# The high parts of the mixers' weight pieces come by a transfer from HBM that casts, and two loads use another queue

## The chip, the cores and the metric

The kernel runs on one core of one Trainium2 chip. TensorE (PE in the profile) multiplies, VectorE (DVE) and ScalarE (ACT) do elementwise work, GpSimd (POOL) does little here besides starting transfers, and SyncE (SP) starts most transfers. Each of these engines has a queue of its own that it works off in order; semaphores join them. The metric is the device time of one execution in microseconds, as the median of several runs; lower is better.

## What is computed

Two layers of a backbone over 256 latent tokens with 256 context tokens ahead of them, 1024 wide. Each layer applies three mixers to one normalised and modulated input `u`, merges them and adds an MLP. Cut to the frame:

```python
for l in range(DEPTH):                      # 2 layers
    u  = rms_norm(h, norm1_g[l]) * (1.0 + sc1) + sh1          # latent, 256 tokens
    uc = rms_norm(hc, norm1_g[l]) * (1.0 + sc1c) + sh1c       # context, 256 tokens
    a_x, a_g, b_q, b_f, b_i, b_o, c_qkv, m_g = split_projection(u @ w_in[l])
    ya = rglru_branch(a_x, a_g, ...)        # gated linear recurrence
    yb = hgrn2_branch(b_q, b_f, b_i, b_o, ...)
    yc = neighbourhood_attention(axial_rope(q_l), axial_rope(k_l), v_l, ..., na_rpb[l])
    h = h + gt1 * merge_branches(ya, yb, yc, m_g, w_branch[l], w_out[l])
    h = h + gt2 * sq_relu_ffn(rms_norm(h, norm2_g[l]) * (1.0 + sc2) + sh2, ffn_w1[l], ffn_w2[l])
    # the context stream takes the same steps in all layers but the last
return h
```

All inputs are float32, and the products are wanted in close to float32 accuracy.

## The kernel before

**Weights.** All weights of the matrix products are packed in HBM as 296 pieces of 128 x 1024 float32 (512 KB), 148 for each layer. A piece passes through three buffers on the chip. `arriving` starts its transfer into `raw` on SyncE's queue (line 211, three buffers). `weights` takes a buffer for the high part `whi` and one for the low part `wlo` (four each), and `split` fills them: ScalarE rounds `raw` to the format that TensorE reads in one pass, `whi` (line 226), and VectorE subtracts, `wlo = raw - whi` (line 227). Each product is then three matmuls with the split input, whi x xhi, whi x xlo and wlo x xhi (`mm3`, lines 240 to 242; in the `tok` pieces lines 1036 to 1038). So the third matmul of a piece is the first that needs `wlo`.

**Pieces and heads.** A layer's mixers are worked off in four heads j = 0 to 3. A head uses ten pieces: `ff` and `fb` (forget gates of hgrn), `hq` (its query), `ax` and `ag` (the linear recurrence's input and gate), `og` (output gate), and `tok` in four parts, tok0 to tok3 (values, and attention's q, k, v). Token tiles and parts of `tok` are worked off in the order of `TOK_UNITS`. The chains that follow the projections (`hgrn`, `attention`, `lru`) are generators in three lanes whose steps are laid between the matmuls of the next head's pieces. Pieces are fetched up to four ahead of the one in use, since there are four `whi` and `wlo` buffers: a new high part can be written as soon as the piece four ahead of it has been used for the last time.

**Order.** The program text gives each piece's steps and a scheduler puts the instructions of each engine in their final order; the queues keep that order. The tables and costs of the planner aren't touched.

**Two other loads.** `opened` in `mixer_pieces` starts, for each head, the load of attention's position bias (`bias`, 512 KB, line 969, on GpSimd's queue but for the very first, on SyncE's) and of the recurrence's gate weights (`gw`, 256 KB, line 977, on GpSimd's queue). `sc` (line 754) first reads the bias.

Of the kernel before, what the change touches and what calls it, by code (L numbers as in the profile page):

```python
# [10 lines left out]
F32 = mybir.dt.float32  # L11
# [5 lines left out]
ALU = mybir.AluOpType  # L17
# [9 lines left out]
NPIECE = 148  # L27
# [9 lines left out]
MIX_ORDER = ("tok", "ff", "fb", "hq", "ax", "ag", "og")  # L37
# [34 lines left out]
def piece_index():  # L72
    idx, n = {}, 0

    def add(key):
        nonlocal n
        idx[key] = n
        n += 1

    for j in range(4):  # L80
        for nm in MIX_ORDER:
            for key in mix_keys(nm, j):
                add(key)
    for _, br, what, i in merge_order(0):
        add((what, br, i))
    for d in range(8):
        add(("out", d))
    for q in range(4):
        for i in range(8):
            add(("f1", q, i))  # L90
    for q in range(4):
        for d in range(8):
            add(("f2", q, d))
    assert n == NPIECE
    return idx


PIECE = piece_index()
# [56 lines left out]
def hybrid_kernel(  # L155
    ctx: ExitStack, tc: tile.TileContext, xT, cT, wpack, ada0w, adaw, lastw, prm, lruw, biasd, consts, cs, gfr, masks, out
):
    nc = tc.nc
# [13 lines left out]
    def two_k(name, dt=F32):  # L172
        return wk.tile([P, T2], dt, tag="t2", name=name, bufs=N2)

    def four_k(name, shape=(2, T2), dt=F32):
        return wk.tile([P] + list(shape), dt, tag="t4", name=name, bufs=N4)
# [32 lines left out]
    def arriving(l, key):  # L209
        raw = wpool.tile([P, 1024], F32, tag="raw", name="raw", bufs=3)  # L210
        nc.sync.dma_start(out=raw, in_=wpack[l * NPIECE + PIECE[key]])
        return raw

    def weights(l, key, raw=None, eng=nc.vector):
        cols = {"tok": 4 * P, "proj": 2 * P}.get(key[0], P)
        raw = arriving(l, key) if raw is None else raw
        lo = wpool.tile([P, 1024], F32R, tag="wlo", name="wlo", bufs=4)
        hi = wpool.tile([P, 1024], F32R, tag="whi", name="whi", bufs=4)
        split(hi, lo, raw, eng=eng)
        v = lambda t: t.rearrange("p (k c) -> p k c", c=cols)  # L220
        return v(hi), v(lo)

    def split(hi, lo, src, scale=None, eng=nc.vector):

        if scale is None:
            nc.scalar.copy(hi, src)  # L226
            eng.tensor_tensor(out=lo, in0=src, in1=hi.bitcast(F32), op=ALU.subtract)  # L227
        else:
            nc.scalar.mul(hi, src, scale)
            nc.vector.scalar_tensor_tensor(  # L230
                out=lo, in0=src, scalar=scale, in1=hi.bitcast(F32), op0=ALU.mult, op1=ALU.subtract
            )
# [86 lines left out]
    def rope_tables(l):  # L319

        for sc in range(2):
            for i, qk in enumerate((1, 0)):
                g = gf[l][:, 2 * sc + qk, :]
                for hd in range(2):
                    for tt in range(2):
                        nc.gpsimd.tensor_tensor(out=ctab[:, sc, tt, i, hd, :], in0=cst[:, sc, tt, :], in1=g, op=ALU.mult)
# [616 lines left out]
    def mixer_pieces(l):  # L943
        T = T2 if l == 0 else TL
        heads = []
        for j in range(4):
            out_pieces = []
            heads.append(out_pieces)
            m = State()
# [6 lines left out]
            def opened(nm, m=m, j=j):  # L956

                if j == 0 and not hasattr(st, "layer" + str(l)):
                    setattr(st, "layer" + str(l), True)
                    st.ys = {}  # L960
                if nm in ("ff", "fb") and not hasattr(m, "TF"):
                    m.TF = four_k("TF")
                if nm == "hq":
                    m.Q = two_k("Q")
                if nm == "tok" and j == 0 and l > 0:
                    rope_tables(l)
                if nm == "tok":
                    m.bias = four_k("bias", (4, TL))
                    (nc.gpsimd if l or j else nc.sync).dma_start(out=m.bias, in_=biasd[l, j])

                    m.tok = [four_k("tok", (2, 2, TL)) for _ in range(2)]
                    m.vtok = lambda c: m.tok[c // 2][:, 0, c % 2]
                if nm == "og" and not hasattr(m, "sog"):
                    m.sog = two_k("sog")
                if nm in ("ax", "ag") and not hasattr(m, "gw"):
                    m.gw = two_k("gw").rearrange("p (a b) -> p a b", b=P)
                    nc.gpsimd.dma_start(out=m.gw, in_=lruw[l, j])
                    m.xc, m.ge = two_k("xc"), two_k("ge")

            def closed(nm, m=m, j=j, lane=lane, chain=chain):  # L980
# [299 lines left out]
    def start():  # L1280
# [23 lines left out]
        def split_part(i, eng=nc.vector):  # L1304
            if i not in st.first and i < 4:
                st.first[i] = weights(0, ("tok", 0, i), first[i], eng)
# [114 lines left out]
    def fetch(n):  # L1421
        while len(ready) < n and pos[0] < len(todo):
            l, key = todo[pos[0]]
            ready.append(weights(l, key))
            pos[0] += 1
# [146 lines left out]
```

## Time and profile before

| what | value |
|---|---|
| time, median of three runs | 1531.65 us (1529.93 to 1533.64) |
| the profiled execution's own time | 1531.65 us |
| its span in the profile | 1529.9 us |
| TensorE busy | 1513.1 us, 99% |
| VectorE busy | 1120.1 us, 73% |
| ScalarE busy | 762.0 us, 50% |
| GpSimd busy | 27.7 us, 2% |
| mean granted TensorE clock | 0.998 |
| read from HBM | 214.74 MB |

The span runs from the first to the last instruction; 1.75 us of the execution's time lie outside it. A busy share is an average over all stages. TensorE is hardly ever idle, so the end of the program is its queue plus what it waits for; the waits and the timeline tell where it does. The mixers of layer 0 lie at about 62 to 400 us, those of layer 1 at about 950 to 1250; merge, output projection and MLP fill the rest.

### The profile page before, as it was taken

The numbers are of one execution on the slowest core, as the hardware profiler recorded it, in microseconds if no ns is written. First come the engines' busy times: TensorE is split into PE (matmuls) and PEld (weight loads), VectorE is DVE, ScalarE is ACT, GpSimd is POOL, SyncE is SP. The second block draws the span as 40 slices with busy tenths as digits, with TensorE's granted clock in tenths as the row PEclk, the third lists the DMA queues.
The fourth block names the chain that finished last, engine by engine and source line by source line (L and its number), as shares of the span: only waits on it lengthen the run. The fifth ranks groups of instructions, "written<-read, shape, count | busy, mean of one in ns | idle before, by whom it ended". The sixth has DMA issues, their size and how long they took to land.

```text
span 1529.9 us, 24126 instructions
## 1 busy us (share of the span) xinstructions
PE 1513.1 (99%) x9521; PEld 1295.8 (85%) x9522; DVE 1120.1 (73%) x2126; ACT 762.0 (50%) x1269; POOL 27.7 (2%) x57
## 2 busy tenths in 40 slices
PE   9999999999999999999999999999999999999999
PEld 5778787777888889888888888878888899999999
DVE  6777768685478898988695856779687766776664
ACT  3467676757333333532322323576777854454442
POOL 1200000020000000000000000000000000000000
PEclk9999999999999999999999999999999999999999
DMA  9412131221273562555464532313323355755553
GB/s 368 156 42 104 56 104 56 69 76 70 83 260 126 205 222 69 179 187 185 162 210 137 193 110 90 124 63 124 103 71 106 109 166 191 266 164 182 186 183 125
DMA packets 61793, 217.36 MB, mean 142 GB/s; under 512 B 7792, under 2 KB 9456, under 8 KB 61680
## 3 DMA queue, kind: packets, MB, share of 16 engines
q1 hardware_dynamic: 59328, 209.88, 40.2%
q0 software_dynamic: 1648, 5.77, 1.2%
q8 instruction: 75, 1.23, 0.3%
q14 instruction: 38, 0.31, 0.1%
q10 hardware_dynamic: 704, 0.17, 0.1%
HBM read 214.74 MB, written 1.05 MB: 141 GB/s over the span
## 4 chain that ended last, share of the span: by engine, by line
PE 90%; DVE 5%; ACT 4%; issue 1%; DMA 1%; SPq 0%; ACTq 0%
PE pd L240 7%; PE pd L242 7%; PE pd L241 7%; PE pf L240 5%; PE pf L242 5%; PE pf L241 5%; PE pg L240 4%; PE pg L241 4%; PE pg L242 4%; PE ptok L1036 3%; PE ptok L1038 2%; PE ptok L1037 2%; PE pp L240 2%; PE pp L241 2%; PE pp L242 2%; PE lv L547 2%
## 5 line engine op out<-in xcount | busy, mean ns | idle before, releaser
L226 ACT CAST whi<-raw 128x1024 fp32r<-128x1024 f32 x296 | 309.6, 1049 | 464.1 <-PE pd L241 155.7
L227 DVE TENSOR_TENSOR wlo<-raw,whi 128x1024 fp32r<-128x1024 f32 x295 | 360.3, 1223 | 151.7 <-ACT whi L226 149.2
L242 PE MATMUL pd<-hhi,wlo 128*128 128x256 f32 (+1 forms) x544 | 177.8, 327 | 0.0
L240 PE MATMUL pd<-hhi,whi 128*128 128x256 f32 (+1 forms) x544 | 177.8, 327 | 0.0
L241 PE MATMUL pd<-hlo,whi 128*128 128x256 f32 (+1 forms) x544 | 177.7, 327 | 0.0
L354 DVE CUSTOM_DVE_ANT_0 junk<-arow,crow 128x1024 bf16<-128x1024 f32 x144 | 173.4, 1221 | 3.4 <-DMA arow<-in_adaw 3.2
L241 PE MATMUL pf<-xlo,whi 128*128 128x256 f32 (+1 forms) x464 | 155.1, 334 | 0.0
L242 PE MATMUL pf<-xhi,wlo 128*128 128x256 f32 (+1 forms) x464 | 155.0, 334 | 0.0
L240 PE MATMUL pf<-xhi,whi 128*128 128x256 f32 (+1 forms) x464 | 155.0, 334 | 0.0
L240 PE MATMUL pg<-xhi,whi 128*128 128x512 f32 (+1 forms) x384 | 131.5, 342 | 0.0
L241 PE MATMUL pg<-xlo,whi 128*128 128x512 f32 (+1 forms) x384 | 129.6, 337 | 0.0
L242 PE MATMUL pg<-xhi,wlo 128*128 128x512 f32 (+1 forms) x384 | 129.2, 337 | 0.0
L1154 DVE SCALAR_TENSOR_TENSOR h<-pd,mod,h 128x256 f32<-128x256 f32 x120 | 55.0, 481 | 80.7 <-PE pd L242 78.7
L241 PEld LDWEIGHTS pd<-hlo,whi 128*128 128x128 f32 x544 | 103.5, 190 | 8.8
L240 PEld LDWEIGHTS pd<-hhi,whi 128*128 128x128 f32 x544 | 103.5, 190 | 8.7
L242 PEld LDWEIGHTS pd<-hhi,wlo 128*128 128x128 f32 x544 | 103.5, 190 | 8.7
L241 PEld LDWEIGHTS pf<-xlo,whi 128*128 128x128 f32 x464 | 88.3, 190 | 8.7
L242 PEld LDWEIGHTS pf<-xhi,wlo 128*128 128x128 f32 x464 | 88.2, 190 | 8.8
L240 PEld LDWEIGHTS pf<-xhi,whi 128*128 128x128 f32 x464 | 88.1, 190 | 8.6
L1036 PE MATMUL ptok<-whi,xhi 128*128 128x512 f32 (+1 forms) x224 | 87.6, 395 | 1.1 <-DVE h L1154 1.1
L1038 PE MATMUL ptok<-wlo,xhi 128*128 128x512 f32 (+1 forms) x224 | 85.0, 379 | 1.6 <-DVE wlo L227 1.6
L1037 PE MATMUL ptok<-whi,xlo 128*128 128x512 f32 (+1 forms) x224 | 84.6, 378 | 0.2 <-DVE xlo L463 0.2
(329 smaller groups left out, 3271.7 us busy)
## 6 DMA issues: line engine op xcount, KB each, us to landing
raw<-in_wpack SPq DMA_DIRECT2D x296, 512.0 KB, 3.5
arow<-in_adaw SPq DMA_DIRECT2D x72, 512.0 KB, 4.7
a<-in_ada0w SPq DMA_DIRECT2D x16, 512.0 KB, 10.4
araw<-in_lastw SPq DMA_DIRECT2D x8, 512.0 KB, 6.4
bias<-in_biasd POOLq DMA_DIRECT2D x7, 512.0 KB, 6.6
h<-in_xT SPq DMA_DIRECT2D x4, 512.0 KB, 5.5
gw<-in_lruw POOLq DMA_DIRECT2D x8, 256.0 KB, 2.9
out<-h SPq DMA_DIRECT2D x8, 128.0 KB, 1.9
```

The source lines that it names most:

```text
L226: nc.scalar.copy(hi, src)
L227: eng.tensor_tensor(out=lo, in0=src, in1=hi.bitcast(F32), op=ALU.subtract)
L240: nc.tensor.matmul(d, lhsT=whi[:, k, :], rhs=xhi, start=(k == 0), stop=False)
L241: nc.tensor.matmul(d, lhsT=whi[:, k, :], rhs=xlo, start=False, stop=False)
L242: nc.tensor.matmul(d, lhsT=wlo[:, k, :], rhs=xhi, start=False, stop=(k == nk - 1))
L354: nc.vector.tensor_tensor_reduce(out=junk, in0=raw, in1=crow[s], scale=1.0, scalar=0.0, op0=ALU.mult, op1=ALU.add, accum_out=section_of(l, ...
L547: nc.tensor.matmul(dst, lhsT=lhs(b), rhs=rhs(b), start=True, stop=True)
L1036: nc.tensor.matmul(dst, lhsT=xhi[:, k, tsl], rhs=whi[:, kk, :], start=(k == 0), stop=False)
L1037: nc.tensor.matmul(dst, lhsT=xlo[:, k, tsl], rhs=whi[:, kk, :], start=False, stop=False)
L1038: nc.tensor.matmul(dst, lhsT=xhi[:, k, tsl], rhs=wlo[:, kk, :], start=False, stop=(k == KD - 1))
L1154: nc.vector.scalar_tensor_tensor(out=h[:, d, sl], in0=p_[:, sl], scalar=mods(l, section, s)[:, d:d + 1], in1=h[:, d, sl], op0=ALU.mult, op ...
```

## The change

For the mixers' pieces of all heads but the first of layer 0, `weights` no longer calls `split`. GpSimd's queue starts a transfer that reads the same 512 KB from HBM once more and writes `whi`, of the other type, so that the transfer casts. VectorE's subtraction stays; it now waits for two transfers instead of one transfer and ScalarE. These are 30 pieces in layer 0 and 40 in layer 1, 70 of 296. Besides, all loads of `bias` and `gw` are started on SyncE's queue. The new lines shift the line numbers behind them by 5: the subtraction in the mixers is L222, the one in `split` L232, the third matmul in `tok` L1043.

```diff
--- before.py
+++ after.py
@@ -216,7 +216,12 @@
         raw = arriving(l, key) if raw is None else raw
         lo = wpool.tile([P, 1024], F32R, tag="wlo", name="wlo", bufs=4)
         hi = wpool.tile([P, 1024], F32R, tag="whi", name="whi", bufs=4)
-        split(hi, lo, raw, eng=eng)
+        if key[0] in MIX_ORDER and (l, key[1]) > (0, 0):
+
+            nc.gpsimd.dma_start(out=hi, in_=wpack[l * NPIECE + PIECE[key]])
+            eng.tensor_tensor(out=lo, in0=raw, in1=hi.bitcast(F32), op=ALU.subtract)
+        else:
+            split(hi, lo, raw, eng=eng)
         v = lambda t: t.rearrange("p (k c) -> p k c", c=cols)
         return v(hi), v(lo)
 
@@ -966,7 +971,7 @@
                     rope_tables(l)
                 if nm == "tok":
                     m.bias = four_k("bias", (4, TL))
-                    (nc.gpsimd if l or j else nc.sync).dma_start(out=m.bias, in_=biasd[l, j])
+                    nc.sync.dma_start(out=m.bias, in_=biasd[l, j])
 
                     m.tok = [four_k("tok", (2, 2, TL)) for _ in range(2)]
                     m.vtok = lambda c: m.tok[c // 2][:, 0, c % 2]
@@ -974,7 +979,7 @@
                     m.sog = two_k("sog")
                 if nm in ("ax", "ag") and not hasattr(m, "gw"):
                     m.gw = two_k("gw").rearrange("p (a b) -> p a b", b=P)
-                    nc.gpsimd.dma_start(out=m.gw, in_=lruw[l, j])
+                    nc.sync.dma_start(out=m.gw, in_=lruw[l, j])
                     m.xc, m.ge = two_k("xc"), two_k("ge")
 
             def closed(nm, m=m, j=j, lane=lane, chain=chain):
```

The change moves instructions, since the scheduler orders the engines anew. Two places on VectorE follow; a name's ending number is the program's own and the same on both sides.

The first is VectorE's queue in layer 1 between heads 0 and 1, where the lows of tok1 (`wlo_9410`) and tok2 (`wlo_9471`) of head 1 are subtracted; `xc` is the recurrence's convolution, `kcT` and `qT` attention's keys and queries, `QQ`, `blk`, `km` and `Tn` belong to hgrn, `ge` is the gate's GELU. Before:

```order
L227 TENSOR_TENSOR wlo_9410<-raw_9408,whi_9411 128x1024 [waits DMAHW1_49,Activation_49]
L924 SCALAR_TENSOR_TENSOR xc_9343<-xpre_9403,prb_83,xc_9343 128x2x254 [waits Activation_49]
L230 SCALAR_TENSOR_TENSOR kcT_9427<-kqT_9430,prb_83,kcT_9427 128x256 [waits Activation_49]
L924 SCALAR_TENSOR_TENSOR xc_9343<-xpre_9403,prb_83,xc_9343 128x2x255 [waits DVE_49]
L230 SCALAR_TENSOR_TENSOR qT_9429<-kqT_9430,qg8_654,qT_9428 128x256 [waits Activation_49]
L924 SCALAR_TENSOR_TENSOR xc_9343<-xpre_9403,prb_83,xc_9343 128x2x255 [waits DVE_49]
L560 COPY km_9457<-KK_9363 128x256
L598 TENSOR_TENSOR QQ_9364<-QQ_9364,TF_9171 128x128x2 [waits PE_49]
L601 COPY_PREDICATED blk_9370<-msk_76,lv_9451 128x128
L611 TENSOR_TENSOR Tn_9461<-TF_9171 128x512
L227 TENSOR_TENSOR wlo_9471<-raw_9469,whi_9472 128x1024 [waits DMAHW2_49,Activation_49]
L934 SCALAR_TENSOR_TENSOR ge_9344<-ge_9344,gpre_9463 128x256 [waits Activation_49]
```

Now:

```order
L929 SCALAR_TENSOR_TENSOR xc_9343<-xpre_9403,prb_83,xc_9343 128x2x254 [waits Activation_49]
L929 SCALAR_TENSOR_TENSOR xc_9343<-xpre_9403,prb_83,xc_9343 128x2x255 [waits DVE_49]
L235 SCALAR_TENSOR_TENSOR kcT_9427<-kqT_9430,prb_83,kcT_9427 128x256 [waits Activation_49]
L929 SCALAR_TENSOR_TENSOR xc_9343<-xpre_9403,prb_83,xc_9343 128x2x255 [waits DVE_49]
L222 TENSOR_TENSOR wlo_9410<-raw_9408,whi_9411 128x1024 [waits DMAHW3_49,DMASW3_49]
L235 SCALAR_TENSOR_TENSOR qT_9429<-kqT_9430,qg8_654,qT_9428 128x256 [waits Activation_49]
L565 COPY km_9457<-KK_9363 128x256
L603 TENSOR_TENSOR QQ_9364<-QQ_9364,TF_9171 128x128x2 [waits PE_49]
L606 COPY_PREDICATED blk_9370<-msk_76,lv_9451 128x128
L616 TENSOR_TENSOR Tn_9461<-TF_9171 128x512
L222 TENSOR_TENSOR wlo_9471<-raw_9469,whi_9472 128x1024 [waits DMAHW6_49,DMASW4_49]
L939 SCALAR_TENSOR_TENSOR ge_9344<-ge_9344,gpre_9463 128x256 [waits Activation_49]
```

The low of tok1 moved behind three steps of the convolution and `kcT`, and its wait is for two transfers; the low of tok2 stays between `Tn` and `ge`, with a wait for two transfers instead of one and ScalarE.

The second is VectorE's queue on the way into layer 1, where the lows of tok1 to tok3 of head 0 are `wlo_8328`, `wlo_8334` and `wlo_8340`; `ut` and `xlo` are the modulated input and its low part, `r_g110` and `r_g111` the two token groups' norm scales, `sums` the sum of squares, line 1154 the addition to the residual `h` (now 1159). Before:

```order
L227 TENSOR_TENSOR wlo_8328<-raw_8326,whi_8329 128x1024 [waits DMAHW5_49,Activation_49]
...
L459 SCALAR_TENSOR_TENSOR ut_8290<-h_84,A_g110_8217,rst_8259 128x256
L420 TENSOR_TENSOR sums_7882<-sums_7882,sqt_8295 128x256 [waits Activation_49]
L1154 SCALAR_TENSOR_TENSOR h_84<-pd_8050,mod0_85,h_84 128x256 [waits PE_49]
L463 SCALAR_TENSOR_TENSOR xlo_7881<-ut_8290,mod1_86,xhi_7880 128x256 [waits Activation_49]
L227 TENSOR_TENSOR wlo_8334<-raw_8332,whi_8335 128x1024 [waits DMAHW6_49]
L420 TENSOR_TENSOR sums_7882<-sums_7882,sqt_8323 128x256 [waits Activation_49]
L227 TENSOR_TENSOR wlo_8340<-raw_8338,whi_8341 128x1024 [waits DMAHW7_49]
L488 TENSOR_SCALAR r_g111_8399<-nss_8396 128x2 [waits PE_49]
```

Now:

```order
L1159 SCALAR_TENSOR_TENSOR h_84<-pd_8050,mod0_85,h_84 128x256 [waits PE_49]
L468 SCALAR_TENSOR_TENSOR xlo_7881<-ut_8286,mod1_86,xhi_7880 128x256 [waits Activation_49]
L468 SCALAR_TENSOR_TENSOR xlo_7881<-ut_8290,mod1_86,xhi_7880 128x256 [waits Activation_49]
L425 TENSOR_TENSOR sums_7882<-sums_7882,sqt_8323 128x256 [waits Activation_49]
L222 TENSOR_TENSOR wlo_8328<-raw_8326,whi_8329 128x1024 [waits DMAHW5_49,DMASW7_49]
L222 TENSOR_TENSOR wlo_8334<-raw_8332,whi_8335 128x1024 [waits DMAHW6_49,DMASW0_49]
L222 TENSOR_TENSOR wlo_8340<-raw_8338,whi_8341 128x1024 [waits DMAHW7_49,DMASW1_49]
L493 TENSOR_SCALAR r_g111_8399<-nss_8396 128x2 [waits PE_49]
```

The low of tok1 moved from the first norm scale, ahead of all `ut` and `xlo` of the first group, to the place directly behind the last `sums`, where the other two follow it without anything between.

## Rows read from the trace of the kernel before

L12 is line 12 of the kernel before. A group of instructions on the page reads: line, engine, operation, out<-in with partitions x elements and type, xcount | busy us, mean ns of one | idle us of the engine just ahead of them, and what ended most of it. In the timeline a bracket gives the idle time ahead of an instruction and what ended it.

**Rows 1.** The page: span; engines' busy time; the cast and the subtraction (columns below).

```profile
span 1529.9 us, 24126 instructions
...
PE 1513.1 (99%) x9521; PEld 1295.8 (85%) x9522; DVE 1120.1 (73%) x2126; ACT 762.0 (50%) x1269; POOL 27.7 (2%) x57
...
L226 ACT CAST whi<-raw 128x1024 fp32r<-128x1024 f32 x296 | 309.6, 1049 | 464.1 <-PE pd L241 155.7
L227 DVE TENSOR_TENSOR wlo<-raw,whi 128x1024 fp32r<-128x1024 f32 x295 | 360.3, 1223 | 151.7 <-ACT whi L226 149.2
```

**Rows 2.** Busy time by stretch: one layer 1 head; the sum over nine mixer stretches.

```profile
core 0: us, PE busy (x) PEld busy (x) DVE busy (x) ACT busy (x) POOL busy (x), PEclk, DMA share, GB/s
...
1060.00:1123.00 63.00, 62.11 (x409) 51.68 (x407) 49.61 (x116) 44.88 (x82) 1.07 (x2) 1.00 0.29 94
...
sum 638.00, PE 631.88 PEld 520.96 DVE 472.73 ACT 429.73 POOL 14.33; mean PE 70.21 PEld 57.88 DVE 52.52 ACT 47.75 POOL 1.59
```

**Rows 3.** TensorE's waits, 965 to 1250: us in total, times, longest.

```profile
PE ptok L1038 <- DVE wlo L227: 1.6, 3, 0.5
PE tp L793 <- ACT s L769: 1.0, 3, 0.3
```

**Rows 4.** Timeline, layer 0: ScalarE's cast, TensorE's wait (start, us, engine, line, operation).

```profile
276.70 1.05 ACT L226 CAST whi<-raw 128x1024 fp32r<-128x1024 f32 x1 [0.93 <-PE ptok L1037]
...
283.61 0.44 PE L793 MATMUL tp<-con,s 128*128 128x128 f32 x2 [1.34 <-ACT s L785]
```

**Rows 5.** Timeline of VectorE: lows of tok2 and tok3 in layer 1.

```profile
1061.86 1.22 DVE L227 TENSOR_TENSOR wlo<-raw,whi 128x1024 fp32r<-128x1024 f32 x1
...
1068.72 1.22 DVE L227 TENSOR_TENSOR wlo<-raw,whi 128x1024 fp32r<-128x1024 f32 x1
```

**Rows 6.** Timeline of ScalarE and TensorE in the same passage.

```profile
1059.17 1.04 ACT L226 CAST whi<-raw 128x1024 fp32r<-128x1024 f32 x1
...
1069.99 0.50 PE L1038 MATMUL ptok<-wlo,xhi 128*128 128x512 f32 x1 [0.55 <-DVE wlo L227]
```

**Rows 7.** DMA issues to landing: windows 881:883, 951:952 and 215:216; then whole span.

```profile
bias<-in_biasd POOLq DMA_DIRECT2D x1, 512.0 KB, 4.3
...
bias<-in_biasd POOLq DMA_DIRECT2D x1, 512.0 KB, 3.8
...
bias<-in_biasd POOLq DMA_DIRECT2D x1, 512.0 KB, 7.9
...
raw<-in_wpack SPq DMA_DIRECT2D x296, 512.0 KB, 3.5
...
bias<-in_biasd POOLq DMA_DIRECT2D x7, 512.0 KB, 6.6
```

**Rows 8.** Timeline on the way into layer 1: VectorE, ScalarE, TensorE.

```profile
954.72 1.22 DVE L227 TENSOR_TENSOR wlo<-raw,whi 128x1024 fp32r<-128x1024 f32 x1
955.85 0.42 DVE L420 TENSOR_TENSOR sums<-sums,sqt 128x256 f32<-128x256 f32 x1
...
954.50 0.42 ACT L418 ACTIVATE sqt<-h 128x256 f32<-128x256 f32 x1 [0.28 <-DVE h L1154]
...
955.03 0.40 PE L1038 MATMUL ptok<-wlo,xhi 128*128 128x512 f32 x1
```

**Rows 9.** Timeline around ff: heads 0 and 1 of layer 1.

```profile
966.76 1.05 ACT L226 CAST whi<-raw 128x1024 fp32r<-128x1024 f32 x1 [0.26 <-PE ptok L1037]
...
972.38 0.40 PE L242 MATMUL pff<-xhi,wlo 128*128 128x512 f32 x1
...
1025.46 1.06 ACT L226 CAST whi<-raw 128x1024 fp32r<-128x1024 f32 x1
...
1032.40 0.40 PE L242 MATMUL pff<-xhi,wlo 128*128 128x512 f32 x1
```

**Rows 10.** Timeline: a bias is issued and first used.

```profile
1099.10 0.53 POOL L969 DMA_DIRECT2D bias<-in_biasd  x1 [11.01 <-DVE ltau L882]
...
1127.42 0.42 DVE L754 CUSTOM_DVE_ANT_0 sc<-sc,bias 128x256 f32<-128x256 f32 x1
```

## The prediction

> **What bounds the kernel now.** I read the page first. TensorE is busy 1513.1 of the 1529.9 us span, so nothing but work on its own queue or an idle stretch ahead of a matmul can move the time [rows 1]. The two operations that the change touches are off that queue: ScalarE's rounding of a piece takes 1049 ns and VectorE's subtraction 1223 ns [rows 1]. Both numbers are large in sum, 70 x 1.049 = 73.4 us of ScalarE's time in the 70 pieces concerned, and neither says anything about the end of the program, since ScalarE is busy half of the span.
>
> So the second view is the busy time by stretch, over the stretches in which the mixers run. The reader is to see how little there is to win: TensorE's busy time is 631.88 of 638.00 us, hence 6.1 us idle in all eight heads and the way into layer 1, at full granted clock (1.00) in each row [rows 2]. VectorE in one layer 1 head is busy 49.61 of 63 us, ScalarE 44.88, so on average both have room [rows 2]. The average hides the place that matters, and the third view, TensorE's waits, names it: in layer 1 there are three waits of 0.5 us for a low part (matmul line L1038 waits for wlo), and three short ones for the softmax activation on ScalarE, 1.0 us together [rows 3]. In layer 0 the one wait of size is for ScalarE, 1.34 us ahead of 283.61 [rows 4]. A low part is late in layer 1, then, once in each of three passages from a head to the next.
>
> The fourth view is the timeline of VectorE in such a passage, 1055 to 1070. From tok2's low to tok3's its operations stand back to back. The low of piece tok2 starts at 1061.86, that of tok3 at 1068.72, and TensorE starts its matmul on the latter at 1069.99 after an idle 0.55 us [rows 5, 6]. Everything that pushes VectorE back between these points pushes TensorE back by the same amount.
>
> **The change part by part.** *Removed:* 70 casts on ScalarE. Where ScalarE ends a wait, this gives time back. In layer 0 the cast at 276.70 takes 1.05 us ahead of the activations that TensorE then waits for [rows 4]. At most that 1.3 us comes back, at least nothing, because VectorE's own results feed the same activations; I take 1.0, the length of the cast. In layer 1 the three waits on ScalarE sum to 1.0 us, and I count none of it, since they come behind the low of tok3 and move with it.
>
> *Added:* 70 transfers of 512 KB on GpSimd's queue, each started when the slot of the high part is free, and a wait for it in front of VectorE's subtraction. Today the high part is there 1.05 us after its slot is free; from now on it is there after D, the time from issue to landing. Behind the waiting subtraction, VectorE's whole queue stands. No row of before shows a casting transfer. The nearest rows are the position-bias loads, the same 512 KB, the same queue, without a cast: 3.8 and 4.3 us for the two that ran alone, 6.6 as the median of seven, the other five of which were issued beside weight pieces, and 7.9 at worst; weight pieces of the same size on SyncE's queue have a median of 3.5 [rows 7]. I take D = 4.3, the longer of the two that ran alone: in the passages the raw piece has landed well ahead of the slot, so that few other bytes move, but a cast is not likely to make it shorter. The ends 3.5 and 6.6 are kept, and 7.9 as the tail.
>
> Where does D cost? For each of the 70 pieces I compared the moment when the slot comes free with the moment when TensorE needs the low part. What hides D and the subtraction (4.3 + 1.2 = 5.5 us) is the work on the pieces fetched before, and nearly everywhere it is longer. Three places are tight.
>
> (a) Piece tok2 in layer 1. ScalarE starts its cast at 1059.17, right when the slot is free (the last matmul of the ag piece on it has just gone), and VectorE starts the low at 1061.86 [rows 5, 6]. The order of VectorE in the changed kernel keeps this low in its place, directly behind Tn and ahead of ge. So with D the subtraction starts at 1059.17 + D, later than now by D - 2.69. At 4.3 that is 1.6 us, at 3.5 it is 0.8, at 6.6 it is 3.9. VectorE is not idle from there to the low of tok3, so TensorE's wait at 1069.99 grows by that. Three passages have this form (heads 0 to 1, 1 to 2, 2 to 3): 3 x 1.6 = +4.8 us.
>
> (b) The way into layer 1. The low of tok1 was done early, between two parts of the scale for the norm. In the new order it stands behind all of them, together with the lows of tok2 and tok3, next to the second scale. TensorE uses it at 955.03 [rows 8]. VectorE reaches the place where it now stands at 954.72 at the latest; without the 1.22 us of the moved subtraction that is 953.5, plus the sum of 0.42 us that now precedes it, so it ends at about 953.5 + 0.4 + 1.2 = 955.1, 0.1 us late. If that sum has to wait for ScalarE's square, which starts at 954.50 and ends at 954.9 in this trace, it ends at about 954.9 + 0.4 + 1.2 = 956.5, late by 1.4. I take +0.7, the middle.
>
> (c) The first piece of the hgrn projections (ff). In head 0 of layer 1 the cast starts at 966.76 and TensorE needs the low at 972.38; the path with D is 966.76 + 4.3 + 1.2 = 972.3, hidden with nothing to spare. In heads 1 to 3 it is 1025.46 + 5.5 = 1031.0 against 1032.40, hidden by 1.4 us [rows 9]. At D = 6.6 this cover is gone: 2.2 us in head 0 and 0.9 in each of the other three, 4.9 in all.
>
> *Moved:* the bias and gate-weight loads go from GpSimd's queue to SyncE's. A bias is issued at 1099.10 and first used at 1127.42, and the gate weights have as much ahead of them [rows 10]; on SyncE's queue they stand among the raw pieces of the same head, each of 3.5 us, so they cost nothing. The cover is the rest of the head's projections on TensorE; without it the price is one load, 6.6 us [rows 7]. *Traffic:* 70 x 0.524 = 36.7 MB more from HBM. In a layer 1 head 10 x 0.524 MB in 63 us is 83 GB/s beside today's 94, and the DMA engines are busy 0.29 of that stretch [rows 2]; doubled, it stays under 0.6. Zero, but it lengthens D when a raw piece is in flight.
>
> The sum: -1.0 + 4.8 + 0.7 + 0 = +4.5 us on the profiled execution. That one took 1531.65 us, 1.75 more than its span, and is also the median of the three runs (1529.93 to 1533.64), so it needs no correction: 1536.1 us.
>
> One rule of the Trainium skill speaks against a D of 4.3. "DMA: Bandwidth & Descriptors", section "Anatomy of one DMA — SWDGE (gpsimd) path", gives a transfer on this path a fixed 2.0 us and bytes over 436 GB/s; for 512 KB this is an estimate of 3.2 us, and the sum by it would be -1.0 + 3 x 0.5 + 0.7 = +1.2 us. No load of this size on that queue is that short here (3.8 and 4.3 alone) [rows 7], so the rows decide; 1532.9 us, which the rule gives, lies in the no-change case below.
>
> **The rivals.** *No change.* If a casting transfer lands like a raw piece does, 3.5 us, place (a) costs 3 x 0.8 = 2.4 and the sum is -1.0 + 2.4 + 0.7 = +2.1: 1533.8 us, within what a measurement of this kernel can't tell from no change (0.2%, 3.1 us). For it speaks that the raw pieces are the same bytes; against it, every bias row [rows 7].
>
> *Faster.* The mechanism: the high part is there before VectorE comes to the low of tok2, so VectorE no longer waits anywhere for ScalarE, and ScalarE, freed of 10 casts in each 63 us, ends its softmax activations earlier. It decides at D = 2.7 us in place (a), or later if VectorE itself arrives later than now. Then the three waits for the lows (1.6 us) and those for ScalarE (1.0 and 1.3) go: -3.9 us, 1527.7 us; no more than the 6.1 us of idle time can come back. Against it: no 512 KB row lands within 2.7 us. For it: ScalarE's freed time reaches further than I can follow by hand.
>
> *Slow transfer.* If casting, or the raw pieces beside it, makes D the 6.6 us of the bias median, (a) costs 3 x 3.9 = 11.7, (c) 4.9, (b) 0.7, less 1.0: +16.3, 1548 us. At 7.9 the same terms are 15.6, 3.5 + 3 x 2.2 = 10.1, 0.7 and -1.0: +25.4, 1557 us. For it speaks that a cast touches every element; against it, that the passages are quiet.
>
> That the change doesn't do what it says can be left out: the new order has 70 transfers into whi on GpSimd's queue and 70 casts fewer on ScalarE.
>
> **How the numbers follow.** Forecast (D from 3.8 to 5.5) 0.35, no change 0.32, faster 0.15, slow transfer 0.18. The forecast's case lies almost wholly beyond 0.2%; a little of it falls within and a little of the no-change case beyond, which cancel. So faster 0.15, same 0.34, slower 0.51. For the range: down to 1527, which takes in most of the faster case and leaves out the one in which more than these waits go; up to 1552, D of about 7.2, which leaves the tail of the slow case out. Its own range for the likeliest case, D from 3.8 to 5.5: (a) 3.3 to 8.4, (b) 0.7, (c) 0 to 1.1, less 1.0, is +3.0 to +9.2 us, 1534.7 to 1540.9.
>
> **What would show it.** Right: in the waits of the changed kernel TensorE's L1038 (now L1043) waits some 2 us for wlo three times in layer 1; VectorE's low of tok2 waits for a transfer there; the transfers into whi take about 4.3 us; the 1.3 us wait at 283.61 is gone. Wrong: VectorE never waits for a transfer in layer 1 (then the no-change or faster case), or waits for it in layer 0 or at pieces ff as well (then the slow one), or TensorE's matmuls themselves get longer, which no term here has.

## The result, and the profile after

| | before | after |
|---|---|---|
| median | 1531.14 us (1529.93 to 1533.64) | 1548.14 us (1543.38 to 1548.55) |
| ratio, 95% interval | | 1.0102 (1.0078 to 1.0125) |
| span of the profiled execution | 1529.9 us | 1541.6 us |
| ScalarE busy | 762.0 us | 698.0 us |
| idle time of TensorE in the nine mixer stretches | 6.1 us | 14.6 us |

The change makes the kernel slower by about 1%. The profiled execution is the quickest of the four after (1543.38 us), so the trace explains 11.7 us of a loss of 12 to 19.

The page of the changed kernel, to be read beside [rows 1]: ScalarE's casts are 226 instead of 296, the 70 lows of the changed pieces stand on a line of their own (L222), and their line names the transfer as what ended the idle time ahead of them. TensorE's busy time has hardly moved (1513.1 before); the span has.

```profile
span 1541.6 us, 24163 instructions
...
PE 1514.8 (98%) x9521; PEld 1296.0 (84%) x9522; DVE 1120.4 (73%) x2126; ACT 698.0 (45%) x1199; POOL 56.5 (4%) x112
...
L231 ACT CAST whi<-raw 128x1024 fp32r<-128x1024 f32 x226 | 236.8, 1049 | 420.3 <-PE pd L246 152.1
...
L222 DVE TENSOR_TENSOR wlo<-raw,whi 128x1024 fp32r<-128x1024 f32 x70 | 85.0, 1220 | 37.4 <-DMA whi<-in_wpack 22.5
...
whi<-in_wpack POOLq DMA_DIRECT2D x70, 512.0 KB, 4.4
```

The same two stretch lines as in [rows 2]. The kernel is later by now, so the first stretch doesn't hold quite the same work, but the sum over the same 638 us does nearly: TensorE's busy time falls from 631.88 to 623.40 us, ScalarE's by 66 us, and the DMA engines' share in a head's stretch rises from 0.29 to 0.48.

```profile
1060.00:1123.00 63.00, 60.05 (x397) 50.20 (x396) 49.58 (x116) 36.29 (x71) 5.26 (x10) 1.00 0.48 161
...
sum 638.00, PE 623.40 PEld 511.22 DVE 468.69 ACT 363.83 POOL 45.09; mean PE 69.27 PEld 56.80 DVE 52.08 ACT 40.43 POOL 5.01
```

TensorE's waits in layer 1, to be read beside [rows 3]. A line gives the sum in microseconds, the number of waits and the longest. The waits for the low of a `tok` piece have grown from 1.6 to 3.6 us in sum, and there are new waits, 1.2 us in sum each, for results of VectorE that have nothing to do with a weight piece: `ks` of hgrn, `qT` of attention.

```profile
PE ptok L1043 <- DVE wlo L222: 3.6, 3, 1.2
PE lv L552 <- DVE ks L534: 1.2, 2, 0.9
PE sc L751 <- DVE qT L235: 1.2, 3, 0.5
PE tp L798 <- ACT s L774: 1.0, 3, 0.3
```

VectorE's waits over the whole span name the source: 21 waits for a casting transfer, up to 3.3 us long, and 7 for which the profile shows no releaser.

```profile
DVE wlo L222 <- DMA whi<-in_wpack: 22.5, 21, 3.3
...
DVE wlo L222 <- issue: 5.2, 7, 1.7
```

These two lines don't hold all of it. Of the 37.4 us of idle time that the page gives ahead of these 70 lows, 36.5 us, in 32 waits, end within 0.1 us behind the landing of the low's own transfer; the 7 without a releaser are among them, and so are four that the view puts down to TensorE, which ended something at the same moment. Ahead of the same 70 lows VectorE had stood idle for 16.9 us in the kernel before.

To see where the time went, the start of each of TensorE's matmuls in the trace of after was set against the same matmul of before. The lag grows as follows (us; the place is the time in the trace of before):

| up to | after | queues only | layer 0 only | layer 1 only | layer 1 without tok2 | five buffers |
|---|---|---|---|---|---|---|
| 60, start-up | 0.5 | 0.1 | 0.2 | 1.0 | 2.7 | 0.1 |
| 320, layer 0's mixers | 4.5 | 0.1 | 2.1 | 1.0 | 2.7 | -0.8 |
| 985, way into layer 1 | 5.4 | 0.1 | 2.4 | 3.9 | 5.8 | -1.4 |
| 1255, layer 1's mixers | 12.7 | 0.0 | 2.3 | 10.1 | 12.8 | -1.0 |
| 1525, end | 11.2 | 0.0 | 0.8 | 8.6 | 11.3 | -2.0 |

The columns behind the first belong to experiments below. Two amounts in it aren't the change: what stands in the first row (loading at the start, which no edit here touches, differs from execution to execution), and what all but one of the columns get back at 1340 to 1360, where the execution of before, and not they, lost some clock (1.0 to 1.5 us, below). For after there remain 4.0 us in layer 0, about 1 on the way into layer 1 and 7.3 in layer 1.

### The profile page after: what moved, and what is told of

Read it like the earlier page. It is cut to its first block, busy times and chain, and to the rows that moved or that the text cites. A ratio compares the mean times of both kernels' runs of the same rounds, so it can differ in the third digit from the quotient of the medians.

```text
span 1541.6 us, 24163 instructions
## 1 busy us (share of the span) xinstructions
PE 1514.8 (98%) x9521; PEld 1296.0 (84%) x9522; DVE 1120.4 (73%) x2126; ACT 698.0 (45%) x1199; POOL 56.5 (4%) x112
## 4 chain that ended last, share of the span: by engine, by line
PE 69%; issue 16%; DVE 7%; DMA 4%; ACT 2%; POOL 1%; POOLq 0%; SPq 0%; DVEq 0%; ACTq 0%
PE pd L245 7%; PE pd L247 7%; PE pd L246 7%; PE pf L245 5%; PE pf L247 5%; PE pf L246 5%; PE pg L245 4%; PE pg L247 4%; PE pg L246 4%; DMA whi<-in_wpack 4%; PE pp L246 2%; PE pp L247 2%; PE pp L245 2%; DVE wlo L222 1%; PE ptok L1012 1%
## 5 line engine op out<-in xcount | busy, mean ns | idle before, releaser
L231 ACT CAST whi<-raw 128x1024 fp32r<-128x1024 f32 x226 | 236.8, 1049 | 420.3 <-PE pd L246 152.1
L232 DVE TENSOR_TENSOR wlo<-raw,whi 128x1024 fp32r<-128x1024 f32 x225 | 275.2, 1224 | 133.9 <-ACT whi L231 132.4
L222 DVE TENSOR_TENSOR wlo<-raw,whi 128x1024 fp32r<-128x1024 f32 x70 | 85.0, 1220 | 37.4 <-DMA whi<-in_wpack 22.5
L1043 PE MATMUL ptok<-wlo,xhi 128*128 128x512 f32 (+1 forms) x224 | 84.5, 378 | 3.6 <-DVE wlo L222 3.6
```

The source lines that it names most:

```text
L222: eng.tensor_tensor(out=lo, in0=raw, in1=hi.bitcast(F32), op=ALU.subtract)
L1043: nc.tensor.matmul(dst, lhsT=xhi[:, k, tsl], rhs=wlo[:, kk, :], start=False, stop=(k == KD - 1))
```

## The experiments

Theory A: the casting transfer comes too late. It can't start before a slot of the high part is free, and it takes some 4 us where ScalarE took 1; VectorE's subtraction waits for it at the head of an in-order queue, and all that stands behind it comes late. Theory B: the moved loads. Theory C: the second reading of the weights. Theory D: the new order of VectorE's queue by itself.

**The queue change alone.**

```diff
-                    (nc.gpsimd if l or j else nc.sync).dma_start(out=m.bias, in_=biasd[l, j])
+                    nc.sync.dma_start(out=m.bias, in_=biasd[l, j])
-                    nc.gpsimd.dma_start(out=m.gw, in_=lruw[l, j])
+                    nc.sync.dma_start(out=m.gw, in_=lruw[l, j])
```

> Only the two loads (bias, gw) move to SyncE's queue; ScalarE casts all pieces as before. Theory A (VectorE's queue stands still until casting transfers land): nothing to wait for here, so 1531 us, within 1.5 us of the kernel before. Theory B (the moved loads, 768 KB per head on the raw pieces' queue, are what delays things): raw pieces and high parts late, 4 us or more slower, 1535 or above.

Measured: 1531.67 us, ratio 0.9996 (0.9986 to 1.0006), and a lag within 0.2 us all the way. The two loads cost nothing on the other queue. Theory B falls as a cause by itself.

**The casting transfers alone.** The change without the lines above, so that `bias` and `gw` stay on GpSimd's queue.

> The 70 casting transfers alone; bias and gw stay on GpSimd's queue, where the casting transfers now stand too. Theory A: as slow as the full change, 11 to 17 us over the kernel before (1542 to 1548); the transfers beside bias and gw take as long as there (6 to 7 us for the og pieces), since the bytes move at the same time from either queue. Theory B: 5 us over at most (1536). A third way: bias and gw wait for buffers in the middle of GpSimd's queue and hold the casting transfers behind them, then it is slower than the full change, above 1550.

Measured: 1542.48 us, ratio 1.0071 (1.0053 to 1.0089): slower by 8 to 14 us. So the casting transfers make the loss, together with the order that the scheduler made for them (VectorE's is that of the full change but for a few instructions), and the loads don't hold them up on GpSimd's queue. One part was missed: the transfers of the og pieces, for which 6 to 7 us were expected, take 3.7 to 5.4 us in layer 1 here. Whether the full change (1.0078 to 1.0125) is really some microseconds worse than this one can't be said: the intervals overlap.

**Layer 0 only, layer 1 only.**

```diff
-        if key[0] in MIX_ORDER and (l, key[1]) > (0, 0):
+        if key[0] in MIX_ORDER and l == 0 and key[1] > 0:
```

> Casting transfers for the 30 pieces of layer 0 only; the loads moved as in the change. Theory A, from the lag of TensorE's matmuls against the kernel before at the end of layer 0's mixers in the trace of the changed kernel (4.6 us): 1535 to 1537. The prediction's own term for layer 0 was -1.0: 1530.

Measured: 1535.84 us, ratio 1.0025 (1.0012 to 1.0039).

```diff
-        if key[0] in MIX_ORDER and (l, key[1]) > (0, 0):
+        if key[0] in MIX_ORDER and l == 1:
```

> Casting transfers for the 40 pieces of layer 1 only; the loads moved as in the change. Theory A, from the growth of the lag from the start of layer 1's mixers to their end (4.6 to 12.7 us): 8 us over, 1538 to 1541. The prediction's own terms for layer 1 (4.8 and 0.7): 1536.6. If the lags of the two layers only add in part, this and the layer 0 kernel together give less or more than the full change.

Measured: 1542.66 us, ratio 1.0071 (1.0052 to 1.0090). Layer 0 costs 2 to 6 us where the prediction had a gain of 1; layer 1 costs 8 to 14 where it had 5.5. Their sum, 0.96%, is about the full change's 1.02%.

**Layer 1 without the tok2 pieces.** The prediction put 4.8 of its 5.5 us on three pieces. Here they alone go back to ScalarE.

```diff
-        if key[0] in MIX_ORDER and (l, key[1]) > (0, 0):
+        if key[0] in MIX_ORDER and l == 1 and (key[1] == 0 or key[0] != "tok" or key[2] != 2):
```

> As the layer 1 kernel, but the tok2 pieces of heads 1 to 3, on which the prediction put 4.8 of its 5.5 us for layer 1, are cast by ScalarE again: 37 casting transfers; VectorE's order is the same in both kernels. By the prediction's term the loss of layer 1 all but goes: 1532 to 1533. If the loss is made at the lows ahead of tok2 (ag, og, tok0, tok1), where VectorE's queue stands up to 3 us for a transfer, it stays: 1539 to 1543, as the layer 1 kernel (1542.7).

Measured: 1543.05 us, ratio 1.0063 (1.0041 to 1.0085); the lag grows by 7.0 us from 985 to 1255, as against 6.2 with tok2. The order of VectorE is the same in both kernels. So the loss doesn't hang on those three pieces.

**Each casting transfer twice**, one behind the other into the same buffer.

```diff
             nc.gpsimd.dma_start(out=hi, in_=wpack[l * NPIECE + PIECE[key]])
+            nc.gpsimd.dma_start(out=hi, in_=wpack[l * NPIECE + PIECE[key]])
```

> The changed kernel with each casting transfer made twice into the same buffer, the second when the first has landed, so that D, from issue to landing, goes from a median of 4.4 to about 8 us; nothing else is changed. Theory A (the loss is D less what hides it, at each low that stands in VectorE's queue): the loss grows far more than in proportion, since more lows lose their cover: 1570 or above. If the loss comes from the new order or from taking ScalarE's casts away, it stays at 1543 to 1548; if from traffic alone, it about doubles, 1555 to 1562.

Measured: 1606.89 us, ratio 1.0483 (1.0452 to 1.0514). More than the transfers changed: the scheduler put some 250 of VectorE's 2126 instructions elsewhere. From the first issue to the last landing it is now 8.8 us in the median (5.0 to 14.6), twice the 4.4 of the change, and the loss goes from 12 to 19 us to 74: more than in proportion, as theory A has it. In its waits VectorE stands 87 us for the transfers instead of 22 (97 instead of 37 us of idle time ahead of the 70 lows in all), and now TensorE itself waits for the high part (lines are shifted by one):

```profile
DVE wlo L223 <- DMA whi<-in_wpack: 87.2, 46, 6.5
...
PE ptok L1042 <- DMA whi<-in_wpack: 9.3, 3, 4.0
PE pff L246 <- DMA whi<-in_wpack: 8.9, 4, 4.0
```

About 20 us of the loss are clock, an estimate: TensorE's busy time is 1536.4 us here, 21.6 more than in the change, at a mean granted clock of 0.988, and some stretches go down to 0.84 (see the last section).

**Five buffers for the high part.** The room comes from the work buffers of 4 KB, 12 instead of 13, and two controls show what that does.

```diff
-        hi = wpool.tile([P, 1024], F32R, tag="whi", name="whi", bufs=4)
+        hi = wpool.tile([P, 1024], F32R, tag="whi", name="whi", bufs=5)
-N2, N4 = 25, 13
+N2, N4 = 25, 12
```

> The kernel before with 12 instead of 13 work buffers of 4 KB: the control for the next three, which need the room. Every theory: 1531 us, within 2.

Measured: 1532.37 us, ratio 1.0000 (0.9991 to 1.0010).

> The changed kernel with 12 work buffers: the second control. Every theory: like the full change, 1542 to 1548.

Measured: 1543.95 us, ratio 1.0076 (1.0061 to 1.0091).

> The changed kernel with five whi buffers instead of four, so that a casting transfer can start one piece (some 6 us of TensorE's work) earlier; the orders of the engines stay. Theory A (the transfer starts too late because the slot comes free too late, and VectorE's queue stands still for it): VectorE's waits for whi, 27.7 us in the trace of the changed kernel, fall to under 3 us, and the time is at most that of the kernel before: 1526 to 1532. Theory C (the second reading of 36.7 MB from HBM and GpSimd's descriptors slow everything whatever the lead): it stays at 1540 or above. Theory D (the new order of VectorE's queue costs by itself): some 1534 to 1537.

Measured: 1531.9 us, ratio 0.9994 (0.9982 to 1.0005). The loss is gone, with the same bytes and the same casts, and the transfers start one piece earlier. That rules out theory C as the cause. It doesn't rule out theory D, since the orders didn't stay as was expected: some 260 of VectorE's 2128 instructions stand elsewhere than in the changed kernel with 12 work buffers. The low of og of head 1 in layer 1 is one of them; in the change it stands behind `Q` and costs most there (next section), here it stands ahead of the rotations (L708) and of `Q`, and its transfer is issued 8 us ahead of it:

```profile
1037.73 0.53 POOL L221 DMA_DIRECT2D whi<-in_wpack  x1 [5.39 <-PE pff L247]
...
1046.05 1.22 DVE L222 TENSOR_TENSOR wlo<-raw,whi 128x1024 fp32r<-128x1024 f32 x1
...
1049.24 0.41 DVE L911 SCALAR_TENSOR_TENSOR Q<-Q,phq 128x256 f32<-128x256 f32 x1
```

So this run doesn't tell how much the earlier transfers brought and how much the new order. The page and the waits of this kernel:

```profile
span 1528.4 us, 24202 instructions
...
PE 1510.6 (99%) x9521; PEld 1294.4 (85%) x9522; DVE 1122.5 (73%) x2126; ACT 700.8 (46%) x1199; POOL 56.8 (4%) x112
```

```profile
DVE wlo L222 <- DMA whi<-in_wpack: 12.8, 8, 4.3
...
PE ptok L1043 <- DVE wlo L222: 2.1, 3, 1.0
```

Another part of the expectation was missed: VectorE's waits for a transfer didn't all but vanish; 12.8 us of them are left in this view, and 17.2 us of its idle time ahead of the 70 lows end with the landing of the low's own transfer. TensorE waits only 2.1 us for lows and doesn't lag, so most of those waits stood where VectorE had time to spare. A wait's length alone doesn't tell its price.

> The kernel before (ScalarE casts) with five whi buffers and 12 work buffers: the control for the five buffers alone. Theory A: 1530 to 1533, as the changed kernel with five buffers (1531.9), since in both the high parts are ready ahead of the lows' places. If the fifth buffer alone is worth 5 us or more, it is 1527 or less, and then the casting transfer still costs that much with five buffers.

Measured: 1534.58 us, ratio 1.0007 (0.9996 to 1.0018). The fifth buffer alone, whose order is much nearer to that of the last kernel (some 90 of VectorE's instructions differ), gives the kernel before nothing, so it doesn't hide a remaining price of the transfers; with it, the casting kernel is 2.7 us ahead by the medians and the intervals still overlap. No version here beats the kernel before by more than the measurement can tell.

**The traffic alone.** The transfers run into a buffer that nobody reads; all casts stay.

```diff
-            nc.gpsimd.dma_start(out=hi, in_=wpack[l * NPIECE + PIECE[key]])
-            eng.tensor_tensor(out=lo, in0=raw, in1=hi.bitcast(F32), op=ALU.subtract)
+            junk = wpool.tile([P, 1024], F32R, tag="wjunk", name="wjunk", bufs=1)
+            nc.gpsimd.dma_start(out=junk, in_=wpack[l * NPIECE + PIECE[key]])
+            split(hi, lo, raw, eng=eng)
```

> The 70 casting transfers run, but into a buffer that nobody reads; ScalarE casts all pieces as before, the loads moved as in the change. Theory A: nothing waits for them, 1531 to 1533. Theory C: the traffic alone makes raw pieces, bias and gw late, 1536 or above.

Measured: 1536.82 us, ratio 1.0037 (1.0022 to 1.0053): by the number theory C's outcome. The trace says otherwise. With no slot to wait for, the transfers run back to back from the start of the program until 350 us, ahead of the one subtraction that GpSimd does for the first pieces, and TensorE waits for that:

```profile
23.45 0.53 POOL L222 DMA_DIRECT2D wjunk<-in_wpack  x1 [6.79 <-DMA wjunk<-in_wpack]
24.08 2.95 POOL L233 TENSOR_TENSOR wlo<-raw,whi 128x1024 fp32r<-128x1024 f32 x1
...
27.08 0.80 PE L1013 MATMUL ptok<-wlo,xhi 128*128 128x512 f32 x1 [3.57 <-POOL wlo L233]
```

The lag is 7.0 us at 60, 8.0 at 320 and 9.3 at 352, and doesn't grow behind that. The DMA share is 0.63 in the stretch below, and the idle time of the mixer stretches is 7.2 us, about that of before:

```profile
150.00:230.00 80.00, 79.95 (x520) 63.37 (x520) 56.57 (x110) 53.91 (x100) 9.01 (x18) 1.00 0.63 195
...
sum 638.00, PE 630.75 PEld 518.71 DVE 486.72 ACT 432.66 POOL 42.59; mean PE 70.08 PEld 57.63 DVE 54.08 ACT 48.07 POOL 4.73
```

So in layer 0 the bytes cost at most 2.3 us, with 56 transfers beside its mixers where the change has 30, and the 7.0 us are an artefact of how this experiment was built. Layer 1 is not tested by it, since no transfer is left to run there. The five buffers are the cleaner test of the bytes.

**The lows on GpSimd.** Casts on ScalarE, the loads moved, and the 70 lows off VectorE.

```diff
-        split(hi, lo, raw, eng=eng)
+        split(hi, lo, raw, eng=nc.gpsimd if key[0] in MIX_ORDER and (l, key[1]) > (0, 0) else eng)
```

> No casting transfers: ScalarE casts as before, bias and gw on SyncE's queue, and the lows of the same 70 pieces are subtracted on GpSimd (its one subtraction of this size in the kernel before takes 2.34 us) instead of VectorE, which is rid of 85 us and of every wait for a high part. If TensorE's waits in the mixers hang on VectorE's queue, it gains at most the 6 us of idle time: 1526 to 1530. If the 1.1 us more for each low, or GpSimd and VectorE getting in each other's way, weigh more: 1533 or above.

Measured: 1593.81 us, ratio 1.0396 (1.0376 to 1.0417), 61 us slower. Some 20 us of that are clock, an estimate (0.985 in the mean; TensorE is busy 22.6 us longer than before). VectorE has 70 subtractions fewer, 85 us of work, and is busy longer than before (1164.3 us, before 1120.1):

```profile
PE 1535.7 (96%) x9521; PEld 1307.5 (82%) x9522; DVE 1164.3 (73%) x2056; ACT 762.6 (48%) x1269; POOL 200.7 (13%) x112
```

In the timeline a subtraction on GpSimd and an operation on VectorE that takes 0.69 us elsewhere ran beside each other, and the latter took 2.32:

```profile
129.37 2.38 POOL L227 TENSOR_TENSOR wlo<-raw,whi 128x1024 fp32r<-128x1024 f32 x1 [24.91 <-ACT whi L226]
...
129.97 2.32 DVE L594 TENSOR_TENSOR KK<-KK,aux 128x512 f32<-128x512 f32 x1 [1.03 <-PE lv L547]
```

It tells nothing about theory A, since VectorE itself got slower. It does say that the lows can't be moved there.

**What the trace of the change itself says of theories A and D.** In layer 1's mixers TensorE's lag grows by 7.3 us, 5.7 of them at eight matmuls that wait for `qT`, `ks` or a low of tok3. Followed back along VectorE's queue without a gap, each of them leads to one of four lows that stood for their transfers, at 1002.62, 1060.59, 1125.51 and 1190.42, for 1.24, 3.30, 2.15 and 1.74 us. In layer 0 the two new waits for hgrn's normalised output (0.64 and 0.78 us) lead back to lows that stood 2.65 and 2.75 us for transfers of 7.7 and 6.7 us. That is theory A at work. Theory D is at work too, at least on the way into layer 1 (place (b) below). What the new order would cost if every transfer landed in time, no run shows.

## Why the prediction was right, and where it was wrong

The direction and the range held: slower, 1548.1 us within 1527 to 1552. The size didn't follow from the sum: 4.5 us were forecast and 12 to 19 measured. That the slow rival had 1548 us is a coincidence of numbers, for it needed D = 6.6 us at tok2 and ff, and in layer 1 D was 3.6 to 4.4 there. The range reaches up to 1552 only for that rival's sake, so that it holds 1548 is luck; the forecast's own 1534.7 to 1540.9 was missed.

Of the prediction's four signs of being right one came, transfers of about 4.3 us. TensorE waits 1.2 us three times for a low where some 2 us were named, no low of tok2 waits for a transfer, and the wait at 283.61 is not gone. One of its signs of being wrong did come: VectorE waits for transfers in layer 0 and at ff (2.53 us in head 0). Two small sums don't come out either: (b) is late by 1.5 us at its end, not 1.4, and the cases' chances add up to 0.53 for slower and 0.32 for the same, not 0.51 and 0.34.

*The bound.* Right. TensorE's work is unchanged, and 8.5 of the 11.7 us of the trace are idle time in the mixer stretches.

*The time from issue to landing.* Right in the median, not where it counted. 4.3 was taken, 4.4 is the median of the 70, 3.6 the least, 7.7 the most. The two loads that it was taken from hadn't run quite alone, a raw piece and a `gw` load overlapped with them [rows 7]. The four lows of layer 1 that cost time had transfers of 5.3, 7.2, 5.9 and 5.9 us; with 4.3 each they would have stood for 0.2 to 0.5 us, an estimate by subtraction. So "few other bytes move" failed there.

*ScalarE's stall in layer 0, -1.0.* It didn't come back. The wait of 1.34 us [rows 4] is 0.80 now, and the lag falls by 0.99 us at this matmul, but two matmuls that stood ahead of the wait stand behind it now, and the lag is 4.6 us at 282 as it is at 285.

```profile
287.26 1.24 PE L798 MATMUL tp<-con,s 128*128 128x128 f32 x6 [0.80 <-ACT s L790]
```

And layer 0 lost 4.0 us net, where the prediction had no loss at all.

*The three tight places.* This is the step that failed. It compared when a slot comes free with when TensorE needs the low part, and called everything else hidden. That asks only whether TensorE has to wait for this low. It leaves out that the low waits at the head of VectorE's queue, and that the operations behind it feed the lanes of hgrn, attention and the recurrence, on which TensorE waits too. The text names that queue ("Behind the waiting subtraction, VectorE's whole queue stands") and then doesn't price it. It is shown by the layer 0 kernel, in which the prediction found no low tight for TensorE and which loses 2 to 6 us, and by the new waits for `ks` and `qT` above, which lead back to lows that stood for transfers.

*Place (a), tok2, +4.8.* The size of a passage was near, the place wrong. From 985 to 1255 the lag of after grows by 7.3 us, but tok2 has no part in it, as the kernel without it shows. In the passage from head 1 to 2, which is also that of the first order shown ahead of the prediction (`wlo_9410` and `wlo_9471` are lows of head 2), its transfer (issued 1067.33) takes 3.6 us and has landed by 1071.0; VectorE comes to the low at 1071.79, later than the transfer, because it is late already.

```profile
whi<-in_wpack POOLq DMA_DIRECT2D x1, 512.0 KB, 3.6
```

```profile
1067.33 0.53 POOL L221 DMA_DIRECT2D whi<-in_wpack  x1 [4.40 <-PE pag L247]
...
1068.82 1.22 DVE L222 TENSOR_TENSOR wlo<-raw,whi 128x1024 fp32r<-128x1024 f32 x1
...
1071.79 1.23 DVE L222 TENSOR_TENSOR wlo<-raw,whi 128x1024 fp32r<-128x1024 f32 x1
...
1078.67 1.22 DVE L222 TENSOR_TENSOR wlo<-raw,whi 128x1024 fp32r<-128x1024 f32 x1
...
1079.94 0.50 PE L1043 MATMUL ptok<-wlo,xhi 128*128 128x512 f32 x1 [1.19 <-DVE wlo L222]
```

What made it late stands 11 us earlier, at the low of og. Its slot is free at 1053.35, the casting transfer is issued then, beside the two moved loads on SyncE's queue, and takes 7.2 us; VectorE is done with Q at 1057.3 and stands 3.30 us. `QQ`, `ks` and four lows come behind.

```profile
1053.35 0.53 POOL L221 DMA_DIRECT2D whi<-in_wpack  x1 [7.62 <-PE pfb L247]
...
1053.22 0.38 SPq L982 DMA_DIRECT2D gw<-in_lruw  x1
1053.65 0.42 SPq L974 DMA_DIRECT2D bias<-in_biasd  x1
...
1056.87 0.42 DVE L911 SCALAR_TENSOR_TENSOR Q<-Q,phq 128x256 f32<-128x256 f32 x1
1060.59 1.23 DVE L222 TENSOR_TENSOR wlo<-raw,whi 128x1024 fp32r<-128x1024 f32 x1 [3.30 <-DMA whi<-in_wpack]
1061.73 0.42 DVE L569 TENSOR_TENSOR QQ<-Q,TF 128x256 f32<-128x256 f32 x1
```

```profile
whi<-in_wpack POOLq DMA_DIRECT2D x1, 512.0 KB, 7.2
bias<-in_biasd SPq DMA_DIRECT2D x1, 512.0 KB, 7.5
gw<-in_lruw SPq DMA_DIRECT2D x1, 256.0 KB, 3.9
```

Before, the low of og was subtracted at 1047.45, ahead of the rotations and of `Q`, and VectorE stood still for none of that passage's lows longer than 0.2 us; [rows 5] show its end. So the low came both to another place and late. The wait of 0.55 us at tok3 [rows 6] did grow, to 1.19, but the rest of the passage's loss had been taken in between, on other waits (0.86 us for `ks`, 0.55 for `qT`).

*Place (b), +0.7.* The size was near, the wait another. The three lows follow the last sum, as the order showed [rows 8], and the lag grows from 4.5 us at 940 to 5.1 at 958 and is 4.8 at 970. But no matmul there waits for a low. Six matmuls that stood ahead of TensorE's wait for the residual `h` stand behind it now, so that it comes to this wait with less done and stands 1.87 us instead of 1.10 (first line, of before, and the line of 958.11). That is a price of the new order, with no transfer in it. *Place (c), ff.* Near: hidden but for 0.23 us that TensorE waits [rows 9].

```profile
954.47 0.50 PE L1036 MATMUL ptok<-whi,xhi 128*128 128x512 f32 x1 [1.10 <-DVE h L1154]
...
958.11 0.50 PE L1041 MATMUL ptok<-whi,xhi 128*128 128x512 f32 x1 [1.87 <-DVE h L1159]
...
958.76 0.41 DVE L425 TENSOR_TENSOR sums<-sums,sqt 128x256 f32<-128x256 f32 x1
959.09 3.49 DVE L222 TENSOR_TENSOR wlo<-raw,whi 128x1024 fp32r<-128x1024 f32 x3
...
960.42 0.49 PE L1043 MATMUL ptok<-wlo,xhi 128*128 128x512 f32 x1
...
977.73 0.50 PE L247 MATMUL pff<-xhi,wlo 128*128 128x512 f32 x1 [0.23 <-DVE wlo L222]
```

*The moved loads and the traffic, 0 each.* Right one by one, by the queue kernel and the five buffers. Together with the casting transfers they aren't quite free, since og's transfer beside them takes 7.2 us where 3.6 is the least; in the kernel without the move the same transfer takes 4.9 us, but that of ag, ahead of it, 7.2 instead of 6.3. How much of the loss that is, stays open, as the kernel without the move is slower too and its interval overlaps.

What also stays open is why the loss in layer 0 is 1.9 us in one trace, 4.0 in another and 6.1 in the one with 12 work buffers, and what the other three runs of after, 5 us longer than the profiled one, lost in addition: there is no trace of them. Their mean granted clock was 0.996 to 0.998 where the profiled run had 1.000, which makes 3 to 6 us of their spans (an estimate), so that most of it may be clock.

## What to carry to other kernels

When a step gets a longer latency, compare its result's arrival not with the moment at which the last consumer needs it but with the moment at which the waiting instruction comes to the head of its in-order queue, and then list what stands behind it and who waits for that. A transfer in place of a 1 us operation may take one buffer more, so that it can start earlier; here it cost 1% with four buffers and nothing with five, though the fifth changed the engines' order too. And relief of an engine that is off the path (here 73 us of ScalarE) brought nothing by itself.

## What the runs showed of the hardware

**The cast didn't lengthen a transfer of this size.** The least of the 70 casting transfers took 3.6 us and 3.7 is common in quiet stretches; loads of the same size and queue without a cast took 3.8 and 4.3 [rows 7]. The estimate of 3.2 us from the Trainium skill ("DMA: Bandwidth & Descriptors", "Anatomy of one DMA — SWDGE (gpsimd) path") was reached by none; beside other transfers it went up to 7.7.

**GpSimd beside VectorE.** In the kernel with lows on GpSimd, VectorE's multiplication `li` (128 x 512, two inputs in SBUF) took 685 ns in the mean before; alone it still takes that, and beside a GpSimd subtraction of 2.4 us up to 2887:

```profile
L877 DVE TENSOR_TENSOR li<-li,ltau x16: 659/688/2887, 136.3 to 1290.2; 128x512 f32<-128x512 f32 x16
```

An operation with an input in PSUM didn't change: the four `ut` (L459, third input in PSUM) that ran beside such a subtraction took 469 to 472 ns, the others 476 in the median. Copies with one input were held up as well: `km` (128 x 256) took 2491 ns in the median of five beside one, and 286 alone. The Trainium skill ("SBUF — State Buffer", "SBUF: two separate sides") says that a GpSimd operation that reads SBUF and a VectorE operation with two SBUF inputs take a shared pair of ports in turn, each for its whole length; the lines of `KK` and `li` agree.

**The granted clock.** Twenty microseconds of the trace of before have 0.91, a mean of the two levels of 1.2 and 2.4 GHz, and its matmuls lose 1.5 us there against the trace of after, which has 1.00. In the 20 us ahead TensorE was busy 18.56; it stood idle for the same time at this place in after, so what decides isn't shown. In the kernel with doubled transfers stretches go down to 0.84, there with TensorE busy 15.96 of the 20 us ahead. So single executions differ by a microsecond or two for each such stretch, on top of the start-up.

```profile
1340.00:1360.00 20.00, 20.00 (x154) 19.89 (x155) 15.25 (x31) 11.14 (x22) 0.00 (x0) 0.91 0.40 121
```

```profile
1120.00:1140.00 20.00, 17.65 (x105) 13.43 (x107) 9.96 (x29) 12.91 (x27) 0.00 (x0) 0.84 0.25 79
```
